# 64 elementwise products of a gated recurrence, on VectorE in place of GpSimd

## The chip, the core and the metric

The kernel runs on one NeuronCore of a Trainium2 chip. The core has a matrix engine (TensorE, PE in the profile; PEld is its weight load), a vector engine (VectorE, DVE), an activation engine (ScalarE, ACT), a general engine (GpSimd, POOL) and a queue engine (SyncE, SP) that here only issues DMA. Each engine works through its own list of instructions in a fixed order and waits on semaphores for the others. The metric is the device time of one execution, in microseconds (us), as the median of several runs.

## The reference

Two transformer blocks on 512 tokens of width 1024: the first with sparse attention, a gating unit and a mixture of experts, the second with stick-breaking attention, a gated linear recurrence and a second mixture of experts. The change lies in the recurrence of the second block. It has 4 heads of 128 and chunks of 128 tokens; cut to what matters:

```
def step(state, inp):
    qc, kc, vc, gc = inp
    bc = jnp.cumsum(gc, axis=2)
    diff = bc[:, :, :, None, :] - bc[:, :, None, :, :]
    decay = jnp.exp(jnp.where(causal, diff, -jnp.inf))
    scores = jnp.einsum('bhtd,bhsd,bhtsd->bhts', qc, kc, decay)
    o = einsum('bhts,bhsv->bhtv', scores, vc) + einsum('bhtd,bhdv->bhtv', qc * jnp.exp(bc), state)
    b_last = bc[:, :, -1, :]
    state = jnp.exp(b_last)[..., None] * state + einsum(
        'bhsd,bhsv->bhdv', kc * jnp.exp(b_last[:, :, None, :] - bc), vc)
    return state, o
```

The decay depends on the pair of positions and on the feature, so the scores are not one product of two matrices.

## The kernel before

The kernel is one program of five stages: first dense part, first experts, second dense part (`dense2`), second experts, final norm. A scheduler turns the Python code into the five lists of instructions; inside `dense2` the string `ORDER` only gives the order in which steps are handed to it, and it interleaves them by its own estimate. All weights come through SP's queue in a fixed order.

The step `L0` to `L3` of `dense2` is the function `levels(h)`, once for each head. It gets the scores of all four chunks (tile `sgf`) from seven products. For a level of half-length B, with `bc` the summed log decay, the tile `x` holds in every first half of 2B positions exp(ref - b) times the key and in every second half exp(b - ref) times the query, where ref is b at the end of the first half. Then x transposed times x holds the wanted scores for all pairs that are split by this level, and a mask picks them. A level is therefore a chain over engines: two subtractions on VectorE (lines 1916 and 1917), one exponential on ScalarE (through `act`, line 1755), two products (lines 1919 and 1920, with `kf` and `hq`), four products of 128x128x128 on TensorE into one PSUM bank (line 1924, tile `lv`; in fp32, so the trace has eight matmuls for four), and a masked copy from the bank into `sgf` on VectorE (line 1925). There is one such bank, so the next level's matmuls wait for this copy; three `x` buffers let the front of the chain run ahead.

After its levels each head makes the decayed queries `qe * q` (line 1930) and the decayed keys `kd * k` (line 1938), transposes the latter (`kt`, lines 1941 and 1942, copied to `kmt` by line 1944), and the step `A0` to `A3` (`across`) carries the state over the chunks. The steps beside it are the attention pairs `P0` to `P3` (`sb_pair`, where GpSimd also has masks, line 2014, and sums, line 2068), projections (`Q`, `G`, `I`; matmuls of lines 146 to 148 into `acc`), and the output product `W0` to `W3` (`back_first`). Each weight tile `wr` is split into a high half `wh` (ScalarE, line 135) and a low half `wl` (VectorE, line 138) before the matmuls may use it. `kmt` of head 1 ends the first half of the levels; levels 2 and 3 run after it without attention beside them.

Of the kernel before, what the change touches and what calls it, by code (L numbers as in the profile page):

```python
# [17 lines left out]
ALU = mybir.AluOpType  # L18
# [3 lines left out]
T = 512  # L22
# [1609 lines left out]
TM = T + NM  # L1632
# [93 lines left out]
def dense2(K, tc, A, router, dump=None):  # L1726

    nc = K.nc
# [8 lines left out]
    with st:  # L1737
# [15 lines left out]
        def act(out, in_, func, **kw):  # L1753

            i = nc.scalar.activation(out, in_, func, **kw)
            if table[0] is not None:
                after(K, i, table[0])
            acts.append(i)
# [7 lines left out]
        def bank(name, tag="ps"):  # L1766
            return (psz if tag == "z" else psp).tile([128, 512], F32, name=name, tag=tag, bufs=BANKS[tag])
# [18 lines left out]
        with tc.tile_pool(name="d2x0", bufs=1, side="right", reuse_waits="tile") as x0:  # L1786
# [18 lines left out]
            q = x0.tile([128, NT, D], F32, name="fq")  # L1805
# [85 lines left out]
        def chunks(ap):  # L1891
            return ap.rearrange("p (c s) -> p c s", s=128)

        def levels(h):

            lf = hp.tile([128, TM], F32, name=f"lf{h}", tag="lf", bufs=1)
            act(lf, sgf[:, h, :], AF.Ln, scale=lb1[:, h:h + 1], bias=lb[:, h:h + 1])
            bc = hp.tile([128, TM], F32, name=f"bc{h}", tag="bc", bufs=2)
            nc.vector.tensor_tensor_scan(bc[:, 0:T], first, lf[:, 0:T], 0.0, op0=ALU.mult, op1=ALU.add)
            nc.vector.tensor_tensor_scan(bc[:, T:TM], first[:, 1:1 + NM], lf[:, T:TM], 0.0, op0=ALU.mult, op1=ALU.add)  # L1900
            q, k = hq[:, h, :], kf[:, h, :]

            S = chunks(sgf[:, h, 0:T])
            ps = bank(f"dg{h}", "lv")
            for c in range(NT):
                s = slice(c * 128, (c + 1) * 128)
                nc.tensor.matmul(ps[:, s], k[:, s], q[:, s], start=True, stop=True)
            nc.vector.tensor_tensor(S, chunks(ps), K.ident[:, None, :].to_broadcast([128, NT, 128]), op=ALU.mult)
            for lg in range(7):
                B = 1 << lg  # L1910
                nb = T // (2 * B)
                v4 = lambda ap: ap.rearrange("p (n two b) -> p n two b", two=2, b=B)
                x = hp.tile([128, T], F32, name=f"x{h}{lg}", tag="X", bufs=3)
                b4, x4 = v4(bc[:, 0:T]), v4(x)
                ref = b4[:, :, 0, B - 1:B].to_broadcast([128, nb, B])
                nc.vector.tensor_tensor(x4[:, :, 0, :], ref, b4[:, :, 0, :], op=ALU.subtract)
                nc.vector.tensor_tensor(x4[:, :, 1, :], b4[:, :, 1, :], ref, op=ALU.subtract)
                act(x, x, AF.Exp)
                nc.gpsimd.tensor_tensor(x4[:, :, 0, :], x4[:, :, 0, :], v4(k[:, 0:T])[:, :, 0, :], op=ALU.mult)
                nc.gpsimd.tensor_tensor(x4[:, :, 1, :], x4[:, :, 1, :], v4(q)[:, :, 1, :], op=ALU.mult)  # L1920
                ps = bank(f"lv{h}{lg}", "lv")
                for c in range(NT):
                    s = slice(c * 128, (c + 1) * 128)
                    nc.tensor.matmul(ps[:, s], x[:, s], x[:, s], start=True, stop=True)
                nc.vector.copy_predicated(S, K.lev[lg][:, None, :].to_broadcast([128, NT, 128]), chunks(ps))

            qe = hp.tile([128, T], F32, name=f"qe{h}", tag="X", bufs=3)
            act(qe, bc[:, 0:T], AF.Exp)
            nc.vector.tensor_copy(ebs[:, h, :], chunks(qe)[:, :, 127])
            nc.gpsimd.tensor_tensor(q, qe, q, op=ALU.mult)  # L1930
            kd = hp.tile([128, T + 32], F32, name=f"kd{h}", tag="kd", bufs=1)
            nc.vector.memset(kd[:, TM:], 0.0)
            c3 = chunks(bc[:, 0:T])
            nc.vector.tensor_tensor(chunks(kd[:, 0:T]), c3[:, :, 127:128].to_broadcast([128, NT, 128]), c3,
                                    op=ALU.subtract)
            nc.vector.tensor_tensor(kd[:, T:TM], bc[:, TM - 1:TM].to_broadcast([128, NM]), bc[:, T:TM], op=ALU.subtract)
            act(kd[:, 0:TM], kd[:, 0:TM], AF.Exp)
            nc.gpsimd.tensor_tensor(kd[:, 0:TM], kd[:, 0:TM], k, op=ALU.mult)
            ps = bank(f"kt{h}", "lv")
            for c in range(NT - 1):  # L1940
                nc.tensor.transpose(ps[:, c * 128:(c + 1) * 128], kd[:, c * 128:(c + 1) * 128], K.ident)
            nc.tensor.transpose(ps[0:32, 384:512], kd[:, T:T + 32], K.ident)
            nc.scalar.activation(k[:, 0:384], ps[:, 0:384], AF.Copy)
            nc.vector.tensor_copy(kmt[:, h, :], ps[0:32, 384:512])
# [240 lines left out]
        for i in range(4):  # L2185
            steps[f"SK{i}"] = lambda i=i: col_meta(SK, lambda b: kT[b], i)
            steps[f"F{i}"] = lambda i=i: col_meta(HF, lambda b: kf[:, b, :], i)
            steps[f"P{i}"] = lambda i=i: sb_pair(i)
            steps[f"L{i}"] = lambda i=i: levels(i)
            steps[f"W{i}"] = lambda i=i: back_first(i)  # L2190
            steps[f"A{i}"] = lambda i=i: across(i)
# [151 lines left out]
```

## Time and profile before

| | us |
|---|---|
| median of 3 runs (1751.13 to 1752.42) | 1751.66 |
| the profiled execution | 1750.18 |
| its span from first to last instruction | 1748.4 |
| PE busy in the span | 1667.2 |
| DVE busy | 813.5 |
| ACT busy | 522.3 |
| POOL busy | 253.8 |

Busy times overlap: all engines run side by side. What lies outside the span (1.8 us) does not depend on the work. PE's busy time counts pipelined matmuls with modelled ends, so it is no measure of how well it is used.

### The profile page before, as it was taken

The numbers are of one execution on the slowest core, as the hardware profiler recorded it, in microseconds if no ns is written. First come the engines' busy times: TensorE is split into PE (matmuls) and PEld (weight loads), VectorE is DVE, ScalarE is ACT, GpSimd is POOL, SyncE is SP. The second block draws the span as 40 slices with busy tenths as digits, with TensorE's granted clock in tenths as the row PEclk, the third lists the DMA queues.
The fourth block names the chain that finished last, engine by engine and source line by source line (L and its number), as shares of the span: only waits on it lengthen the run. The fifth ranks groups of instructions, "written<-read, shape, count | busy, mean of one in ns | idle before, by whom it ended". The sixth has DMA issues, their size and how long they took to land. (4 is left out here: it accounts for less than half of the span.)

```text
span 1748.4 us, 22778 instructions
## 1 busy us (share of the span) xinstructions
PE 1667.2 (95%) x8932; PEld 1094.7 (63%) x8932; DVE 813.5 (47%) x1832; ACT 522.3 (30%) x896; POOL 253.8 (15%) x308
## 2 busy tenths in 40 slices
PE   8999999999999999999899999899999999999976
PEld 6877777787888745454487977688644344333423
DVE  6668865463346823322654378877611111211114
ACT  4333355662334210110425367634300000000012
POOL 0000111110211000000323257550000000000010
PEclk9999999999999999999999999999999999999998
DMA  4422222257334499999531220217499999999995
GB/s 139 134 73 73 73 73 61 60 175 241 95 100 144 184 420 407 420 420 407 218 109 49 73 72 1 73 37 297 187 419 420 419 420 420 418 420 420 419 419 225
DMA packets 112656, 403.72 MB, mean 231 GB/s; under 512 B 21950, under 2 KB 44478, under 8 KB 75936
## 3 DMA queue, kind: packets, MB, share of 16 engines
q1 hardware_dynamic: 101952, 376.60, 55.8%
q0 software_dynamic: 8880, 25.58, 3.8%
q8 instruction: 72, 1.18, 0.3%
q10 hardware_dynamic: 1712, 0.04, 0.1%
q14 instruction: 40, 0.33, 0.1%
HBM read 382.44 MB, written 27.26 MB: 234 GB/s over the span
## 5 line engine op out<-in xcount | busy, mean ns | idle before, releaser
L1533 PE MATMUL gg<-rg,xT 128*64 128x512 f32 x1536 | 372.7, 597 | 9.5 <-DMA rg<-in_w_expert_gate 5.0
L1533 PEld LDWEIGHTS gg<-rg,xT 128*64 128x64 f32 x1536 | 114.3, 136 | 210.6 <-issue 183.3
L1546 PE MATMUL py<-rg,aT 128*64 128x512 f32 x768 | 198.0, 604 | 20.9 <-DMA rg<-in_w_expert_down 20.9
L138 DVE TENSOR_TENSOR wl<-wr,wh 128x1024 fp32r<-128x1024 f32 (+2 forms) x114 | 141.0, 1238 | 136.8 <-ACT wh L135 135.3
L135 ACT ACTIVATE wh<-wr 128x1024 fp32r<-128x1024 f32 (+2 forms) x116 | 119.6, 1033 | 203.7 <-PE acc L148 113.1
L1546 PEld LDWEIGHTS py<-rg,aT 128*64 128x64 f32 x768 | 58.2, 138 | 141.5 <-issue 100.3
L1269 DVE SCALAR_TENSOR_TENSOR sg<-gg,gsl,sg 128x256 f32<-128x256 f32 (+1 forms) x32 | 19.7, 617 | 252.2 <-PE gg L1533 172.7
L146 PE MATMUL acc<-wh,xh 128*128 128x512 f32 (+3 forms) x312 | 121.3, 389 | 2.1 <-DVE xl L272 2.1
L1323 POOL DMA_INDIRECT yd<-ys,to x28 | 27.9, 998 | 655.4 <-DVE ys L1322 505.9
L148 PE MATMUL acc<-wl,xh 128*128 128x512 f32 (+3 forms) x312 | 119.9, 385 | 0.5 <-DVE wl L138 0.5
L147 PE MATMUL acc<-wh,xl 128*128 128x512 f32 (+3 forms) x312 | 118.8, 381 | 0.0
L1113 DVE TENSOR_TENSOR xT<-xp,gT 128x512 f32<-128x512 f32 x56 | 38.6, 690 | 152.7 <-PE xp L1110 150.3
L1280 ACT ACTIVATE aT<-ap 128x256 f32<-128x256 f32 (+1 forms) x32 | 15.7, 490 | 291.1 <-PE ap L1277 291.1
L1321 ACT ACTIVATE ys<-py,gsl 128x512 f32<-128x512 f32 x28 | 19.3, 688 | 257.1 <-PE py L1546 151.1
L1322 DVE TENSOR_SCALAR ys<-py,gsl 128x512 f32<-128x512 f32 x28 | 21.0, 751 | 135.9 <-PE py L1546 135.9
L146 PE MATMUL acc<-xh,wh 128*128 128x512 f32 x192 | 77.5, 404 | 0.0
L147 PE MATMUL acc<-xh,wl 128*128 128x512 f32 x192 | 76.7, 400 | 0.0
L148 PE MATMUL acc<-xl,wh 128*128 128x512 f32 x192 | 76.6, 399 | 0.0
L146 PEld LDWEIGHTS acc<-wh,xh 128*128 128x128 f32 x312 | 59.0, 189 | 17.7 <-issue 4.9
L148 PEld LDWEIGHTS acc<-wl,xh 128*128 128x128 f32 x312 | 59.0, 189 | 11.7 <-DVE wl L138 1.0
L146 PE MATMUL acc<-ah,wh 128*128 128x264 f32 (+1 forms) x192 | 63.6, 331 | 2.5 <-ACT wh L135 2.1
L147 PEld LDWEIGHTS acc<-wh,xl 128*128 128x128 f32 x312 | 59.2, 190 | 10.2
(752 smaller groups left out, 3476.3 us busy)
## 6 DMA issues: line engine op xcount, KB each, us to landing
rg<-in_w_expert_in SPq DMA_DIRECT2D x64, 1024.0 KB, 11.8
rg<-in_w_expert_gate SPq DMA_DIRECT2D x64, 1024.0 KB, 20.3
rg<-in_w_expert_up SPq DMA_DIRECT2D x64, 1024.0 KB, 20.2
rg<-in_w_expert_down SPq DMA_DIRECT2D x62, 1024.0 KB, 20.5
wr<-in_w_in SPq DMA_DIRECT2D x84, 512.0 KB, 3.6
rg<-in_w_expert_out SPq DMA_DIRECT2D x32, 1024.0 KB, 11.4
yd<-zeros POOLq DMA_DIRECT2D x2, 4096.0 KB, 24.9
yb<-yd POOLq DMA_DIRECT2D x14, 512.0 KB, 10.0
```

The source lines that it names most:

```text
L135: self.high = nc.scalar.activation(wh, raw, AF.Copy)
L138: self.low = low.tensor_tensor(wl, raw, f32(wh), op=ALU.subtract)
L146: nc.tensor.matmul(out, ah, bh, start=first, stop=False)
L147: nc.tensor.matmul(out, al, bh, start=False, stop=False)
L148: return nc.tensor.matmul(out, ah, bl, start=False, stop=last)
L1113: nc.vector.tensor_tensor(xT[:, k2 * 2:k2 * 2 + 2, :], ps, gT[:, kk:kk + 2, None].to_broadcast([128, 2, n]), op=ALU.mult)
L1269: K.gated = nc.vector.scalar_tensor_tensor(sg, ps_u, scale, sg, op0=ALU.mult, op1=ALU.mult)
L1321: nc.scalar.activation(y[:, 0:512], py[0], AF.Copy, scale=gate)
L1322: nc.vector.tensor_scalar(y[:, 512:D], py[1], gate, None, op0=ALU.mult)
L1323: nc.gpsimd.indirect_dma_start(yd, bass.IndirectOffsetOnAxis(ap=rows, axis=0), y, None, bounds_check=ROWS - 1, oob_is_err=False)
L1533: in_turn(nc.tensor.matmul(pss[i][64 * s:64 * s + 64, :], xT[kk // 4][:, kk % 4, c0 + 64 * s:c0 + 64 * s + 64], wt[2 * p + s, nm, kk // 4] ...
L1546: m = nc.tensor.matmul(py[q][64 * s:64 * s + 64, :], aT[:, f, 64 * s:64 * s + 64], wt[2 * p + s, second, f // 2][:, f % 2, q * 512:(q + 1) ...
```

## The change

Four lines name `nc.vector` where they named `nc.gpsimd`: 56 products of 128x256 (seven levels, two halves, four heads), four of 128x512 (line 1930) and four of 128x528 (line 1938). The computation is the same.

```diff
                 act(x, x, AF.Exp)
-                nc.gpsimd.tensor_tensor(x4[:, :, 0, :], x4[:, :, 0, :], v4(k[:, 0:T])[:, :, 0, :], op=ALU.mult)
-                nc.gpsimd.tensor_tensor(x4[:, :, 1, :], x4[:, :, 1, :], v4(q)[:, :, 1, :], op=ALU.mult)
+                nc.vector.tensor_tensor(x4[:, :, 0, :], x4[:, :, 0, :], v4(k[:, 0:T])[:, :, 0, :], op=ALU.mult)
+                nc.vector.tensor_tensor(x4[:, :, 1, :], x4[:, :, 1, :], v4(q)[:, :, 1, :], op=ALU.mult)
...
-            nc.gpsimd.tensor_tensor(q, qe, q, op=ALU.mult)
+            nc.vector.tensor_tensor(q, qe, q, op=ALU.mult)
...
-            nc.gpsimd.tensor_tensor(kd[:, 0:TM], kd[:, 0:TM], k, op=ALU.mult)
+            nc.vector.tensor_tensor(kd[:, 0:TM], kd[:, 0:TM], k, op=ALU.mult)
```

Every engine issues the same instructions as before, but for these 64. Their order differs on PE, DVE, ACT and POOL from the first head's levels to the end of the last head's, since the scheduler places the rest anew; SP's list is the same. Two places are shown. On DVE, in head 3, this is a stretch of the levels before the change (`x_10040` to `x_10076` are the tiles of levels 3 to 6, `lv_10034` to `lv_10058` the banks' contents of levels 2 to 4):

```order
L1925 COPY_PREDICATED sgf<-lv_4922,lv_10034 128x512
L1916 TENSOR_TENSOR x_10064<-bc_9995 128x8x32
L1917 TENSOR_TENSOR x_10064<-bc_9995 128x8x32
L138 TENSOR_TENSOR wl_10258<-wr_10255,wh_10257 128x1024
L1925 COPY_PREDICATED sgf<-lv_4923,lv_10046 128x512
L1916 TENSOR_TENSOR x_10076<-bc_9995 128x4x64
L1917 TENSOR_TENSOR x_10076<-bc_9995 128x4x64
L1952 COPY vmh_10313<-hvm 32x64
L1952 COPY vmh_10356<-hvm 32x64 x2
L1925 COPY_PREDICATED sgf<-lv_4924,lv_10058 128x512
```

And this is the same stretch of DVE after the change:

```order
L1925 COPY_PREDICATED sgf<-lv_4922,lv_10034 128x512
L1916 TENSOR_TENSOR x_10064<-bc_9995 128x8x32
L1919 TENSOR_TENSOR x_10052<-x_10052,kf 128x16x16
L1920 TENSOR_TENSOR x_10052<-x_10052,hq 128x16x16
L1917 TENSOR_TENSOR x_10064<-bc_9995 128x8x32
L1925 COPY_PREDICATED sgf<-lv_4923,lv_10046 128x512
L1916 TENSOR_TENSOR x_10076<-bc_9995 128x4x64
L1919 TENSOR_TENSOR x_10064<-x_10064,kf 128x8x32
L1920 TENSOR_TENSOR x_10064<-x_10064,hq 128x8x32
L1917 TENSOR_TENSOR x_10076<-bc_9995 128x4x64
L1925 COPY_PREDICATED sgf<-lv_4924,lv_10058 128x512
```

Between two masked copies DVE now has four instructions of a level, and the split of a weight (`wl_10258`) and the small copies that stood there have moved behind the last level. On PE, in the same head, the matmuls of levels 2 and 3 stood like this before (`acc` rows belong to the projection `I1`):

```order
L1924 MATMUL lv_10034<-x_10028 128x128 x4
L146 MATMUL acc_10106<-wh_10132,ah 128x256
L147 MATMUL acc_10106<-wh_10132,al 128x256
L148 MATMUL acc_10106<-wl_10133,ah 128x256
L146 MATMUL acc_10106<-wh_10132,ah 128x256
L147 MATMUL acc_10106<-wh_10132,al 128x256
L148 MATMUL acc_10106<-wl_10133,ah 128x256
L146 MATMUL acc_10106<-wh_10132,ah 128x256
L147 MATMUL acc_10106<-wh_10132,al 128x256
L1924 MATMUL lv_10046<-x_10040 128x128 x4
```

After the change all seven levels of this head stand together on PE, and the projection goes on behind them:

```order
L147 MATMUL acc_10107<-wh_10132,al 128x256
L1924 MATMUL lv_10010<-x_10004 128x128 x4
L1924 MATMUL lv_10022<-x_10016 128x128 x4
L1924 MATMUL lv_10034<-x_10028 128x128 x4
L1924 MATMUL lv_10046<-x_10040 128x128 x4
L1924 MATMUL lv_10058<-x_10052 128x128 x4
L1924 MATMUL lv_10070<-x_10064 128x128 x4
L1924 MATMUL lv_10082<-x_10076 128x128 x4
L148 MATMUL acc_10106<-wl_10133,ah 128x256
L146 MATMUL acc_10106<-wh_10132,ah 128x256
```

So PE has nothing to do between two levels of head 3, where it had seven to thirteen matmuls before; levels 2 to 5 of head 2 stand together in the same way. The half `wl_10133`, which the first row behind the levels needs, is made on DVE only just before the last masked copy.

## Rows read from the trace of the kernel before

**Rows 1.** Stretches: length; busy PE, PEld, DVE, ACT, POOL; PE clock, DMA share, GB/s.

```profile
1024.70:1124.70 100.00, 95.28 (x648) 69.89 (x646) 85.47 (x163) 71.53 (x144) 66.66 (x96) 1.00 0.12 38
1124.70:1173.50 48.80, 42.35 (x382) 39.92 (x383) 45.11 (x95) 18.22 (x32) 32.74 (x32) 0.97 0.14 44
1173.50:1252.00 78.50, 75.28 (x521) 68.87 (x520) 57.65 (x197) 30.89 (x59) 3.04 (x2) 1.00 0.58 228
1252.00:1748.00 496.00, 456.57 (x2125) 190.63 (x2123) 92.88 (x173) 45.82 (x85) 21.79 (x37) 0.99 0.96 396
1130.00:1140.00 10.00, 6.67 (x47) 6.32 (x47) 10.00 (x14) 4.16 (x6) 8.56 (x8) 0.89 0.18 52
1140.00:1150.00 10.00, 10.00 (x81) 9.64 (x81) 9.32 (x23) 3.00 (x7) 4.92 (x6) 0.94 0.01 2
```

**Rows 2.** A wait of SP's DMA queue, 1185 to 1270: us, times, longest.

```profile
SPq L974 <- PE acc L148: 27.2, 1, 27.2
```

**Rows 3.** Timelines of DVE and, in the last row, of POOL: start, us, engine, line.

```profile
1124.37 0.25 DVE L1944 COPY kmt<-kt 32x128 f32<-32x128 f32 x1
...
1125.64 0.41 DVE L1917 TENSOR_TENSOR x<-bc 128x256 f32<-128x256 f32 x1
1125.97 0.67 DVE L1908 TENSOR_TENSOR sgf<-dg,ident 128x512 f32<-128x512 f32 x1
...
1133.25 2.34 DVE L1899 TENSOR_TENSOR_SCAN bc<-first,lf 128x512 f32<-128x512 f32 x1
...
1137.43 1.20 DVE L138 TENSOR_TENSOR wl<-wr,wh 128x1024 fp32r<-128x1024 f32 x1
...
1171.51 0.75 DVE L1925 COPY_PREDICATED sgf<-lv,lv 128x512 f32<-128x512 uint8 x1 [1.11 <-PE lv L1924]
1173.57 0.74 DVE L1925 COPY_PREDICATED sgf<-lv,lv 128x512 f32<-128x512 uint8 x1 [1.31 <-PE lv L1924]
...
1133.01 1.50 POOL L1938 TENSOR_TENSOR kd<-kd,kf 128x528 f32<-128x528 f32 x1
```

**Rows 4.** Instructions by tile, all four heads: least, median and greatest ns.

```profile
L1916 DVE TENSOR_TENSOR x<-bc x28: 392/410/1119, 1025.1 to 1167.5; 128x256 f32<-128x256 f32 x28
L1917 DVE TENSOR_TENSOR x<-bc x28: 400/486/1221, 1025.4 to 1167.9; 128x256 f32<-128x256 f32 x28
L1919 POOL TENSOR_TENSOR x<-x,kf x28: 719/834/1799, 1027.5 to 1169.6; 128x256 f32<-128x256 f32 x28
...
L1899 DVE TENSOR_TENSOR_SCAN bc<-first,lf x4: 1217/1407/2342, 1023.8 to 1133.2; 128x512 f32<-128x512 f32 x4
...
L1934 DVE TENSOR_TENSOR kd<-bc x4: 659/1085/1333, 1035.7 to 1159.0; 128x512 f32<-128x512 f32 x4
L1936 DVE TENSOR_TENSOR kd<-bc x4: 152/480/824, 1038.3 to 1160.8; 128x16 f32<-128x16 f32 x4
```

**Rows 5.** Groups of DVE, 1124.7 to 1173.5: count, busy us, mean ns, idle before.

```profile
L1917 DVE TENSOR_TENSOR x<-bc 128x256 f32<-128x256 f32 x14 | 9.1, 647 | 0.0
L1916 DVE TENSOR_TENSOR x<-bc 128x256 f32<-128x256 f32 x14 | 6.7, 477 | 0.0
L138 DVE TENSOR_TENSOR wl<-wr,wh 128x1024 fp32r<-128x1024 f32 x4 | 6.0, 1491 | 0.0
L1934 DVE TENSOR_TENSOR kd<-bc 128x512 f32<-128x512 f32 x2 | 2.0, 996 | 0.0
L1936 DVE TENSOR_TENSOR kd<-bc 128x16 f32<-128x16 f32 x2 | 1.5, 766 | 0.0
```

**Rows 6.** The timeline of PE.

```profile
1133.38 0.28 PE L146 MATMUL acc<-wh,ah 128*128 128x256 f32 x1
...
1134.10 0.28 PE L146 MATMUL acc<-wh,ah 128*128 128x256 f32 x1
...
1136.36 1.13 PE L1924 MATMUL lv<-x 128*128 128x128 f32 x8 [1.98 <-DVE sgf L1925]
...
1173.29 0.49 PE L148 MATMUL acc<-wl,ah 128*128 128x256 f32 x2
```

## The prediction

> **What bounds the kernel now.** I read the stretches first. From 1252 us to the end the DMA engines are busy for 0.96 of the time at 396 GB/s and PE for 457 of 496 us [rows 1]: the last experts' weights stream at the rate that the queues give, so this stage ends a fixed time after its stream gets going. The stream can't get going on its own: in SP's queue the loads of the experts' weights stood 27.2 us behind matmuls of the dense stage [rows 2], whose weight buffers they take over. So what moves the end of PE's work in the dense stage moves the end of the kernel by as much, and nothing behind it takes a delay up; from 1173.5 to 1252 PE is busy for 75.3 of 78.5 us. The question is only when PE gets past the last level.
>
> Up to there the reader is to see two halves. In the first, 100 us with the attention pairs beside the levels, no engine is full: PE 95.3, DVE 85.5, ACT 71.5, POOL 66.7. In the second, 48.8 us with levels 2 and 3, DVE is busy for 45.1 and PE for 42.4 [rows 1], and PE's long waits are for the masked copy on DVE, as the 1.98 us ahead of 1136.36 [rows 6]. There DVE sets the time, and the change gives it more to do.
>
> **What DVE takes over.** A product of 128x256 is not on DVE before, but the subtraction is, with two inputs of the same size from SBUF: it takes 0.39 to 0.41 alone, and in a run of them the next begins 0.33 later [rows 3, 4]. The bounds are 0.33, and 0.65 if it were always blocked as the subtraction of line 1917 is on average [rows 5]; with nothing left on POOL in the second half I take 0.33. For 512 elements I take 0.6 (0.659 at least for line 1934 [rows 4], less the same overlap). Each half of the stage gets 28 products of levels and four large ones: 28 x 0.33 + 4 x 0.6 = 11.6 us.
>
> **What DVE gets back.** DVE and POOL hold each other up. The scan of line 1899 took 2.34 us at 1133.25, while POOL worked on decayed keys for 1.50 from 1133.01, where it takes 1.22 alone [rows 3, 4]. In the second half the mean over the least time of each group comes to: line 1917 14 x (0.647 - 0.400) = 3.5; line 1916 14 x (0.477 - 0.392) = 1.2; the four splits 4 x (1.491 - 1.20) = 1.2; the scan 1.1; line 1934 2 x (0.996 - 0.659) = 0.7; line 1936 2 x (0.766 - 0.152) = 1.2 [rows 3 to 5]. That is 8.9 us, and there all of POOL's work is what leaves it, so all of it comes back.
> The Trainium skill says of this ("SBUF — State Buffer", "Who interferes with whom") that a VectorE instruction with two SBUF inputs and a GpSimd instruction that reads SBUF block each other fully, whichever begins second. The trace agrees: 2.34 against 1.22, with 1.26 us of the 1.50 falling into it. By that rule the gain could be as large as all the time that the products were on POOL, and the sum below would come out faster; the rows give the 8.9.
>
> **The first half.** The same 11.6 us come onto DVE. I take the same 8.9 back as in the second half, so DVE has 2.7 us more in a half where it idles for 14.5 [rows 1]; POOL loses about 29 us of work (28 at a median of 0.83 [rows 4] and four of about 1.5 [rows 3]), so masks and sums of the attention pairs no longer queue behind products. PE's order there is nearly the old one. I count this half at nothing; if the idle time can't cover it, it costs 2.7, and more if the products, now in DVE's queue, wait for their exponential with attention work behind them (a rival). If POOL's shorter queue tells, it gains up to 4: of PE's 4.7 idle us little more than that can go.
>
> **The second half.** I sum DVE from the copy to `kmt` that ends at 1124.62 [rows 3] to the moment when PE goes on with `acc` behind the last level, 1173.29 before [rows 6], 48.7 us. In the new order that moment is the end of `wl_10133`, since the first row behind the levels needs it. DVE's work up to there: 45.1 as before, less 8.9, plus 11.6, plus the scan and one operation of 512 that now stand behind `kmt` instead of ahead of it (1.2 + 0.6), less one split that has moved behind the last level (1.2): 48.4. To this come DVE's own waits. A level in the new order is four instructions and the masked copy, 4 x 0.33 + 0.63 = 1.95; but the loop from one copy over PE's eight matmuls to the next copy takes 2.06 even where DVE idles for 1.31 of it (1171.51 to 1173.57 [rows 3]). With 11 such rounds in heads 2 and 3 that is 1.1; and I take 0.9 for the two `across` steps, whose square, root and norm go back and forth to ACT. DVE idles for 3.7 in this half before; 0 and 4 are the bounds of the 2.0. Sum 50.4, that is 1.7 us later than before (bounds -0.3 to +3.7).
>
> At that moment PE has done less than before. Counted in the two orders, the rows ahead of the last level hold 24 fewer matmuls of 128x256 (33 of the projection `I1` fall behind it, 9 come ahead). One is issued every 0.12 us (1133.38 to 1134.10, six steps [rows 6]): 24 x 0.12 = 2.9 us, which PE, full from here on, has to do later. That is the price of the bare block of seven levels: of 2.06 us a level PE works for eight matmuls, about 0.9.
>
> **The clock.** From 1130 to 1140 PE was busy for 6.67 us, and after those waits the granted clock was below full: 0.89 in these 10 us and 0.94 in the next 10 [rows 1], which is one spell at 1.2 in place of 2.4 GHz for (0.11 + 0.06) x 10 / 0.5 = 3.4 us; it costs half of that, 1.7. The new order has two sparse blocks, levels 2 to 5 of head 2 (some 8 us) and all of head 3 (some 14). I count one spell more, 1.7 us; bounds are one less and two more, -1.7 to +3.4.
>
> **Sum**: 0 + 1.7 + 2.9 + 1.7 = 6.3 us on the profiled execution's 1750.2: 1756.5. That execution is 1.5 below the median of the runs, so against the median 1751.7 + 6.3 = 1758.0.
>
> **The rivals.**
> *Nothing to measure.* The first half gains what POOL's queue held up (-4), or the 24 matmuls find their place in gaps behind the levels: 6.3 - 4 = 2.3, 1754. Against the second: PE is busy for 75.3 of 78.5 us there. For the first: POOL was busy for 67 us of 100 and 29 of them leave.
> *Faster.* The levels get shorter, as the change would have it: two products take 0.66 on DVE in a run against 1.44 on POOL at its best (0.719 each [rows 4]), and nothing blocks any more. PE's idle 6.4 us in the second half and the slow spell's 1.7 are what there is to win, 8.1; with half of it and a gain of 2 in the first half the time is 1746. It happens if DVE gets from `kmt` to `wl_10133` in less than 42.3 us (48.7 less the 2.9 of displaced work and the 3.5 of my bound). For it speaks that 14 levels took 48.7 us, 3.5 for each, where a round can take 2.06; against it that DVE's work of 48.4 us alone is more than 42.3.
> The Trainium skill's rule ("GPSIMD Engine Reference", "Performance versus the Vector engine") that VectorE is the engine for elementwise work is on this rival's side, with a factor of 1.96 at 2048 elements. The trace has 1.8 at 256 (0.719 to 0.392), and that this helps only an engine with time left is what the sum above weighs.
> *Slower still.* The products stand in DVE's queue and wait there for their exponential, and in the first half the attention's sums (lines 2006 to 2010 and 2025), on which ScalarE and PE wait, stand behind them. DVE's idle 14.5 us are the cover; with 8 of 28 products late by 0.7 (one exponential) it costs 5.6 more, 1763.6.
>
> **Chances.** Forecast (1755.5 to 1762) 0.42; slower still 0.13; nothing to measure 0.25; faster 0.20. A measurement of this kernel can tell 0.2%, 3.5 us, from no change: faster is below 1748.2, slower above 1755.2; so faster 0.20, same 0.25, slower 0.55. The range takes in the bounds of the first half (-4), the waits and the clock, and reaches into the rivals on both sides: 1747.5 to 1764.5; the forecast's own range is 1755.5 to 1762.
>
> **What would show it.** In the trace after: line 1919 on DVE at 0.39 to 0.41 in the second half, and lines 1916, 1917 and 1899 at their least there; masked copies of head 3 about 2.06 apart with PE idle for about 1 us between its groups; PE going on with `acc` 50 us after `kmt` of head 1, and the end of the `acc` rows 24 matmuls later than that; one or more further stretches with the clock below full. It is wrong if the first half, from the first scan to that `kmt` (100.8 us before), changes by more than 4 us, if the rounds are longer than 2.2 us, or if the experts' stream begins at another distance from the end of the dense stage's matmuls.

## The result, and the profile after

The changed kernel takes 1760.65 us (median of 5 runs, 1758.38 to 1760.71), the kernel before 1751.66 on the same chip: a ratio of 1.0053, with a 95% interval of 1.0042 to 1.0064. By the ratio that is 9.3 us slower, where 6.3 were forecast; the time lies in the forecast's own range, 1755.5 to 1762.

The two profiled spans differ by 10.5 us (1758.9 and 1748.4), but the first scan of the levels, before which nothing was moved, starts at 1025.07 after and at 1023.82 before. So 1.25 us belong to other stages and 9.2 to the change. These are the boundaries in the trace of after, first in the timeline of DVE, then in that of PE (start, us, engine, line).

```profile
1025.07 1.22 DVE L1899 TENSOR_TENSOR_SCAN bc<-first,lf 128x512 f32<-128x512 f32 x1
...
1124.68 0.27 DVE L1944 COPY kmt<-kt 32x128 f32<-32x128 f32 x1
```

```profile
1179.70 0.56 PE L148 MATMUL acc<-wl,ah 128*128 128x256 f32 x1
...
1247.24 0.39 PE L148 MATMUL acc<-wol,m2h 128*128 128x512 f32 x1
...
1263.08 0.65 PE L1533 MATMUL gg<-rg,xT 128*64 128x512 f32 x2
```

They are the first scan, `kmt` of head 1, PE going on behind the last level, the last `acc` matmul of the dense stage and the first matmul of the experts'. In the trace of before, the first scan and those two matmuls are these:

```profile
1023.82 1.22 DVE L1899 TENSOR_TENSOR_SCAN bc<-first,lf 128x512 f32<-128x512 f32 x1
...
1236.81 0.39 PE L148 MATMUL acc<-wol,m2h 128*128 128x512 f32 x1
...
1252.64 0.65 PE L1533 MATMUL gg<-rg,xT 128*64 128x512 f32 x2
```

The stretches of after between its boundaries, and two of 10 us in which the clock was low (the last runs 4.3 us beyond the second stretch), with the columns of [rows 1]:

```profile
1025.10:1124.95 99.85, 95.59 (x648) 69.51 (x647) 87.60 (x188) 69.21 (x142) 39.60 (x64) 1.00 0.10 33
1124.95:1179.70 54.75, 45.97 (x363) 42.12 (x361) 48.44 (x127) 21.05 (x36) 0.00 (x0) 0.86 0.09 30
1179.70:1263.10 83.40, 80.17 (x554) 73.52 (x553) 60.17 (x204) 32.04 (x62) 3.03 (x2) 0.99 0.59 227
1263.10:1758.90 495.80, 455.36 (x2117) 189.38 (x2116) 92.25 (x172) 45.22 (x84) 21.71 (x37) 0.99 0.96 396
1140.00:1150.00 10.00, 8.54 (x37) 7.86 (x38) 6.95 (x16) 2.09 (x4) 0.00 (x0) 0.55 0.08 21
1174.00:1184.00 10.00, 8.18 (x44) 7.54 (x43) 7.68 (x17) 2.10 (x4) 0.00 (x0) 0.66 0.25 68
```

The first half takes 99.9 us (100.8 before), the second 54.7 (48.7 before), the rest of the dense stage from 1179.70 to 1247.24 67.5 (63.5 before, 1173.29 to 1236.81): -0.9, +6.1 and +4.0. Behind that all is as it was: the experts' first matmul follows 15.84 us later (15.83 before, 1236.81 to 1252.64), and the rest takes 495.8 in both. SP's wait, which was 27.2 [rows 2], is nearly as long:

```profile
SPq L974 <- PE acc L148: 26.4, 1, 26.4
```

In the second half the mean granted clock is 0.86, that is (1 - 0.86) x 54.75 / 0.5 = 15.3 us at 1.2 GHz, in two spells: around 1140 to 1150, in head 2's block of levels and behind it (0.55), and from 1175 on, in head 3's and a little beyond (0.66). Before there was one of 3.4 us.

On DVE the products cost what the subtraction costs, and in the second half, where GpSimd has nothing left, nothing is blocked any more. In the first half GpSimd still has the attention's work, and there a product can take 1.40 us (at 1077.82, beside 1.37 of GpSimd from 1077.57). First instructions by tile over all heads (least, median, greatest ns, as in [rows 4]), then the groups of DVE in the second half (as in [rows 5], idle time and its releaser last):

```profile
L1919 DVE TENSOR_TENSOR x<-x,kf x28: 402/417/1403, 1031.0 to 1175.6; 128x256 f32<-128x256 f32 x28
...
L1899 DVE TENSOR_TENSOR_SCAN bc<-first,lf x4: 1214/1224/1225, 1025.1 to 1150.9; 128x512 f32<-128x512 f32 x4
...
L1936 DVE TENSOR_TENSOR kd<-bc x4: 158/166/168, 1040.9 to 1155.8; 128x16 f32<-128x16 f32 x4
```

```profile
L1925 DVE COPY_PREDICATED sgf<-lv,lv 128x512 f32<-128x512 uint8 x13 | 9.5, 730 | 4.9 <-PE lv L1924 4.9
L1917 DVE TENSOR_TENSOR x<-bc 128x256 f32<-128x256 f32 x14 | 5.9, 418 | 0.0
L1920 DVE TENSOR_TENSOR x<-x,hq 128x256 f32<-128x256 f32 x14 | 5.8, 418 | 0.0
L1919 DVE TENSOR_TENSOR x<-x,kf 128x256 f32<-128x256 f32 x14 | 5.8, 418 | 0.1
L1916 DVE TENSOR_TENSOR x<-bc 128x256 f32<-128x256 f32 x14 | 5.8, 413 | 0.0
L138 DVE TENSOR_TENSOR wl<-wr,wh 128x1024 fp32r<-128x1024 f32 x3 | 3.7, 1218 | 0.0
```

The block of head 3 on PE, where a row is now a whole level and nothing stands between two of them:

```profile
1170.98 1.13 PE L1924 MATMUL lv<-x 128*128 128x128 f32 x8 [0.92 <-ACT x L1755]
1173.02 1.13 PE L1924 MATMUL lv<-x 128*128 128x128 f32 x8 [0.92 <-ACT x L1755]
1175.07 2.02 PE L1924 MATMUL lv<-x 128*128 128x128 f32 x8 [0.91 <-DVE sgf L1925]
1178.00 2.05 PE L1924 MATMUL lv<-x 128*128 128x128 f32 x8 [0.91 <-DVE sgf L1925]
```

At full clock eight matmuls span 1.13 us and a round is 2.04; when the clock has fallen they span 2.02 and a round is 2.93. The idle 0.9 in each round stays, so a slow round is 0.89 longer, less than half of its length.

### The profile page after: what moved, and what is told of

The parts are those of the page before. It is cut to its first block, busy times and chain, and to the rows that moved or that the text cites. A ratio compares the mean times of both kernels' runs of the same rounds, so it can differ in the third digit from the quotient of the medians.

```text
span 1758.9 us, 22734 instructions
## 1 busy us (share of the span) xinstructions
PE 1675.9 (95%) x8930; PEld 1101.4 (63%) x8932; DVE 821.0 (47%) x1896; ACT 522.4 (30%) x896; POOL 192.6 (11%) x244
```

## The experiments

**Theory A (bare blocks).** DVE's list is full of products, so the splits of weights (line 138) that the projection needs move behind the levels. PE has nothing to issue between two levels of heads 2 and 3. Matmuls are displaced, and the clock falls. **Theory B (DVE's load).** DVE has more work in front of the last level, and the time follows it, whatever PE has between the levels. Every run is compared with the kernel before on the same chip, over all its runs; ratios carry 95% intervals.

In the first four runs the kernel before has a median of 1751.76 us, in the next four 1752.37, in the last four 1751.24.

**Level products alone.** Of the change, only these two lines:

```diff
-                nc.gpsimd.tensor_tensor(x4[:, :, 0, :], x4[:, :, 0, :], v4(k[:, 0:T])[:, :, 0, :], op=ALU.mult)
-                nc.gpsimd.tensor_tensor(x4[:, :, 1, :], x4[:, :, 1, :], v4(q)[:, :, 1, :], op=ALU.mult)
+                nc.vector.tensor_tensor(x4[:, :, 0, :], x4[:, :, 0, :], v4(k[:, 0:T])[:, :, 0, :], op=ALU.mult)
+                nc.vector.tensor_tensor(x4[:, :, 1, :], x4[:, :, 1, :], v4(q)[:, :, 1, :], op=ALU.mult)
```

> Only the 56 products of the levels (lines 1919 and 1920) go to VectorE; the eight large ones (lines 1930 and 1938) stay on GpSimd. Theory A (bare blocks: DVE's list, filled with products, puts the splits of the weights behind the levels, PE has nothing to issue between them, matmuls are displaced and the clock falls to 1.2 GHz): levels 2 to 5 of head 2 and six of the seven of head 3 still stand together on PE, so nearly all of the loss stays, 7 to 10 us over before, with some 14 us or more at half clock between 1130 and 1190. Theory B (DVE's added work sets the time, whatever stands on PE): 18.5 of the 23.2 us of products move, so 0.8 of the loss of 9, 7 us over before. The two differ in the clock, not in the time.

1763.17 us, ratio 1.0065 (1.0048 to 1.0082): all of the loss and, in the medians, more than that. In its second half the mean clock is 0.90:

```profile
1128.90:1182.40 53.50, 43.60 (x352) 39.70 (x351) 48.05 (x125) 19.76 (x36) 5.08 (x4) 0.90 0.10 30
```

This run shows which lines carry the loss; as expected, it doesn't separate the theories.

**Large products alone.** Of the change, only the other two:

```diff
-            nc.gpsimd.tensor_tensor(q, qe, q, op=ALU.mult)
+            nc.vector.tensor_tensor(q, qe, q, op=ALU.mult)
...
-            nc.gpsimd.tensor_tensor(kd[:, 0:TM], kd[:, 0:TM], k, op=ALU.mult)
+            nc.vector.tensor_tensor(kd[:, 0:TM], kd[:, 0:TM], k, op=ALU.mult)
```

> Only the eight large products (lines 1930 and 1938) go to VectorE. Theory A (bare blocks): PE has 5 to 14 matmuls between two levels of heads 2 and 3 as before, so no long spell at half clock (3.4 us or none) and a time within 2 us of before. Theory B (DVE's added work): 0.2 of the loss of 9, some 2 us over before.

1750.42 us, ratio 0.9992 (0.9983 to 1.0001), and the clock at 1.00 through both halves. As A has it; B's 2 us are outside the interval.

**I1's splits ahead.** The whole change, and in `proj_tok2`, which makes the projections of 256 columns (2816 is I1's first column):

```diff
-        ws.append(W.split(raw, 4, 256))
+        with K.tc.high_priority(offset=URGENT) if extra and c0 == 2816 else ExitStack(): ws.append(W.split(raw, 4, 256))
```

> The whole change, and the two splits of I1's weights (lines 135 and 138) are given to the scheduler with a higher priority, so DVE makes them ahead of head 3's levels; the work is the same. PE's order is that of the change up to head 3, whose levels now have 9 to 18 matmuls of the projection between them. Theory A (bare blocks): the 24 displaced matmuls (2.9 us) and the spell at half clock in head 3 (6.8 us, worth 2.9) come back, head 2's spell stays: some 3.3 us over before, about 1755. Theory B (DVE's added work): DVE has the same work in front of the last level, one split more, so the time stays 9 us over before, or above.

1751.85 us, ratio 1.0003 (0.9993 to 1.0012): nothing is left of the loss that can be measured. B falls, for DVE's work is the same. The stretches (columns as above) from the first scan to `kmt` of head 1, to PE going on, and to the last matmul of the dense stage, then head 2's block:

```profile
1026.20:1126.10 99.90, 95.60 (x648) 69.52 (x648) 87.64 (x188) 69.27 (x143) 39.66 (x65) 1.00 0.10 33
1126.10:1176.40 50.30, 46.76 (x428) 44.03 (x426) 47.98 (x128) 22.92 (x40) 0.00 (x0) 1.00 0.14 43
1176.40:1236.50 60.10, 58.72 (x391) 51.86 (x390) 46.20 (x141) 22.94 (x45) 0.00 (x0) 1.00 0.64 254
1140.00:1150.00 10.00, 7.97 (x63) 7.22 (x62) 9.92 (x22) 2.31 (x4) 0.00 (x0) 1.00 0.07 20
```

The second half is 4.4 us shorter than after the change with DVE as busy (47.98 to 48.44), and what follows is 7.4 shorter, mostly since PE got through 428 matmul records there in place of 363. More came back than expected (8.8 by the ratios for 5.7), because head 2's spell is gone too, in a block that is as bare as it was. That is one trace, and its execution is 2.4 us faster than the median: in the two traces the way from the first scan to the last `acc` matmul is 11.9 us shorter than after the change (210.3 for 222.2), by the ratios 8.8. The mean clock of the whole span is 0.986 to 0.991 in the twelve runs, so in some of them a spell may have come here too.

**The waits filled with idle work.** The whole change, and behind the matmuls of line 1924, for heads 2 and 3 (`dm` is one spare bank for each of these heads):

```diff
+                for c in range(3 if h > 1 else 0): nc.tensor.matmul(dm[:, c * 128:c * 128 + 128], x[:, c * 128:c * 128 + 128], x[:, 0:128], start=True, stop=True)
```

> The whole change, and in heads 2 and 3 each level is followed in the code by three products of 128x128x128 of its own x into a spare bank that nobody reads (42 products added, 84 matmuls, some 9.7 us of PE's time at full clock); DVE's list and the splits are not helped by it. Theory A (bare blocks, by the clock): PE is busy in its waits, the granted clock stays full between 1130 and 1190 (3.4 us or less at half), and 5 to 6 us come back although PE has 9.7 us more to do: some 3 to 4 us over before, 1755. If the loss is displaced work and DVE's alone, nothing comes back, and the time is 9 us over before or more, up to 18 if the added matmuls are on the path.

1755.50 us, ratio 1.0022 (1.0013 to 1.0031). This kernel does 84 matmuls more than the changed one and is 5.4 us faster (1.0053 - 1.0022 = 0.0031 of 1751.7). Its second half and head 2's block:

```profile
1124.80:1175.30 50.50, 49.33 (x458) 46.92 (x457) 48.85 (x129) 21.41 (x37) 0.00 (x0) 1.00 0.14 43
...
1140.00:1150.00 10.00, 10.00 (x85) 9.58 (x84) 9.55 (x23) 3.36 (x6) 0.00 (x0) 1.00 0.17 55
```

The clock stays at 1.00, and those 5.4 us are the nearest that a run comes to its price. This isn't peculiar to the profiled executions: the mean clock of the whole span is 0.985 to 0.987 in all five runs of the changed kernel and 0.989 to 0.992 in all eleven of this one. The other 3.3 that I1's splits gave back (1.0022 to 1.0003) are put down to real work in place of idle work.

**Heads 0 and 1 alone, heads 2 and 3 alone.** In `levels`, with `E` for `nc.gpsimd` in the four lines (and `h > 1` in the second run):

```diff
+            E = nc.vector if h < 2 else nc.gpsimd
```

> The products of heads 0 and 1 go to VectorE (lines 1919, 1920, 1930, 1938 for h < 2), those of heads 2 and 3 stay on GpSimd. Theory A (bare blocks): the second half has 5 to 14 matmuls between two levels as before, the first half has attention beside the levels, so the time is that of before or up to 1 us less: 1750 to 1752.5, and no spell of more than 3.4 us at half clock between 1120 and 1190. Theory B (DVE's added work sets the time wherever it comes): half of the products, half of the loss, some 4.5 us over before.

1755.11 us, ratio 1.0016 (1.0007 to 1.0025): 2.8 us slower, a miss for A as it was put and between the two theories. PE has matmuls between the levels and the clock is 1.00 in the second half, but that half takes 54.4 us:

```profile
1125.20:1179.60 54.40, 45.58 (x410) 42.06 (x408) 45.88 (x101) 21.97 (x39) 33.41 (x32) 1.00 0.16 49
```

The new order of the first half leaves head 2's scan behind `kmt`, as after the change, and here with slow products behind it. The timeline of DVE, and in that of PE the first level's matmuls with the wait ahead of them:

```profile
1124.90 0.27 DVE L1944 COPY kmt<-kt 32x128 f32<-32x128 f32 x1
...
1126.90 1.22 DVE L1899 TENSOR_TENSOR_SCAN bc<-first,lf 128x512 f32<-128x512 f32 x1
```

```profile
1134.07 0.60 PE L1924 MATMUL lv<-x 128*128 128x128 f32 x3 [1.89 <-POOL x L1920]
```

Before, that scan began ahead of `kmt`:

```profile
1123.23 1.22 DVE L1899 TENSOR_TENSOR_SCAN bc<-first,lf 128x512 f32<-128x512 f32 x1
```

So something that A lacked has a price here, and the order that the first half hands on may be it. That it is the late scan is not shown: with the large products alone the scan is behind `kmt` too (1126.87, `kmt` at 1126.38), with slow products behind it, and nothing is lost.

> The other half: the products of heads 2 and 3 go to VectorE, those of heads 0 and 1 stay on GpSimd. The six waits between the levels of head 3 are bare on PE, as in the whole change; between those of head 2 there are 0 to 17 matmuls. Theory A (bare blocks): nearly the whole loss less the spell in head 2, which is shorter or gone: 5 to 9 us over before, with at least one spell at half clock in head 3. Theory B (DVE's added work): half of the loss, some 4.5 us. If the loss arises in the first half, none.

1754.74 us, ratio 1.0020 (1.0011 to 1.0029): 3.5 us slower, less than the 5 to 9 that A expected, while B's 4.5 is inside the interval. The spell in head 3 is there, and longer than after the whole change: the mean clock from 1164 to 1180 is 0.57, which is 13.8 us at half clock. Here head 2's scan is ahead of `kmt` again (1124.67, `kmt` at 1125.81), and the second half takes only 49.3 us:

```profile
1126.10:1175.40 49.30, 42.41 (x357) 39.04 (x357) 45.64 (x121) 17.88 (x31) 0.00 (x0) 0.89 0.07 22
...
1164.00:1180.00 16.00, 12.42 (x57) 11.42 (x58) 11.55 (x26) 3.38 (x6) 0.00 (x0) 0.57 0.16 52
```

Head 3's last four levels run at half clock there. At 0.89 us for each, this half would take about 45.7 us at full clock, 3 less than before (an estimate): the products on VectorE do shorten the levels, and the bare block more than takes that back.

**The control.** The kernel before, with the one line of `proj_tok2` that puts I1's splits ahead.

> A control: the kernel before with nothing but the higher priority of the two splits of I1's weights. Its PE had matmuls between all levels already. Theory A (the splits matter to the change because its DVE list holds them back): no difference beyond 2 us. If the priority is worth something by itself, and what it gave back to the changed kernel was that and not the cure of the bare block, this kernel is 5 to 8 us faster than before.

1752.39 us, ratio 1.0005 (0.9996 to 1.0014). The priority is worth nothing measurable by itself; what it gave the changed kernel was the cure.

**More splits ahead.** The whole change, with the splits of I0 and I1 (in `proj_tok2`) and of W0 and W1 (in `back_first`) put ahead, at twice the priority of the run with I1's alone:

```diff
-        ws.append(W.split(raw, 4, 256))
+        with K.tc.high_priority(offset=1000) if extra and c0 in (2560, 2816) else ExitStack(): ws.append(W.split(raw, 4, 256))
...
-            wh, wl = W.split(W.load(A["w_out_2"][0], g * 256, 256, 0, 4), 4, 256)
+            raw = W.load(A["w_out_2"][0], g * 256, 256, 0, 4)
+            with tc.high_priority(offset=1000) if g in (0, 1) else ExitStack(): wh, wl = W.split(raw, 4, 256)
```

> The whole change with a higher priority (twice that of the run with I1's splits alone) for the splits of I0, I1, W0 and W1. PE has 7 to 30 matmuls between the first levels of head 2 and 9 to 15 between all of head 3; levels 3 to 6 of head 2 stay bare. Theory A (bare blocks): as with I1's splits alone or up to 2 us less: 1749.5 to 1752. Theory B (DVE's added work, or the order of the first half, which moves here too): 1755 or more.

1745.68 us, ratio 0.9968 (0.9958 to 0.9979): faster than both kernels, by more than A expected. Its control is the kernel before with this diff alone:

> A control to the fastest run so far: the kernel before, its products on GpSimd, with the same higher priority for the splits of I0, I1, W0 and W1. If the whole gain comes from the splits, this kernel is some 6 us faster than before too. If it takes both (DVE no longer blocked by GpSimd in levels whose waits are filled), it is within 2 us of before, as with I1's splits alone, since its PE had 4 to 19 matmuls between all levels already.

1752.92 us, ratio 1.0010 (1.0001 to 1.0019). So the gain takes both, the splits ahead and the products on VectorE. The second half with the products on VectorE, its stretch and the waits of PE in it (us, times, longest):

```profile
1126.70:1175.90 49.20, 45.89 (x426) 43.72 (x425) 47.99 (x128) 21.38 (x37) 0.00 (x0) 1.00 0.14 44
```

```profile
PE lv L1924 <- DVE sgf L1925: 1.8, 2, 0.9
PE lv L1924 <- ACT x L1755: 1.5, 2, 0.9
```

And with them on GpSimd:

```profile
1126.50:1177.70 51.20, 43.65 (x392) 40.02 (x392) 45.47 (x95) 19.17 (x33) 30.46 (x32) 1.00 0.14 42
```

```profile
PE lv L1924 <- DVE sgf L1925: 4.7, 4, 1.5
PE lv L1924 <- POOL x L1920: 2.8, 5, 1.2
```

PE waits 3.3 us for levels with the products on VectorE and 7.5 with them on GpSimd, where the subtraction of line 1917 takes 701 ns on average against 418.

Three mixtures were run with the same splits ahead, to see which products make the gain: with `E = nc.vector if h < 2 else nc.gpsimd` as above, with lines 1930 and 1938 alone on VectorE, and with line 1919 alone.

> Products of heads 0 and 1 on VectorE, of heads 2 and 3 on GpSimd, with the higher priority for the splits of I0, I1, W0 and W1. The first half's order is that of the fastest run, the second half has 6 to 26 matmuls in all waits, the four of head 2 that are bare there among them. If bare waits are what is left to win, 2 to 4 us below that run, 1742 to 1744; if DVE is better off without products on GpSimd beside it in the second half, above it, 1747 to 1750.

1750.20 us, ratio 0.9991 (0.9982 to 1.0000).

> Only the eight large products on VectorE, with the higher priority for the splits of I0, I1, W0 and W1. All waits of heads 2 and 3 have 6 to 18 matmuls. If the gain of the fastest run is that of filled waits, it comes here too: 1745 to 1748. If it takes the level products on VectorE, this stays near the run with the large products alone, 1750.

1751.00 us, ratio 0.9992 (0.9983 to 1.0001).

> Of the two products of a level the first (line 1919) on VectorE, the second (line 1920) and the large ones on GpSimd, with the higher priority for the splits of I0, I1, W0 and W1. PE has 3 to 25 matmuls in all waits of heads 2 and 3. If filled waits alone decide, 1744 to 1747. If GpSimd beside DVE costs what the rows of before show (blocking of some 9 us in the second half with two products a level there, half of it with one), 1749 to 1752.

1747.30 us, ratio 0.9978 (0.9969 to 0.9987). In all three every wait of heads 2 and 3 has matmuls in it and the clock is full there. So filled waits are not enough: with the second half's products on GpSimd, or only the large ones on VectorE, nothing measurable is won. With one of two on VectorE the gain is two thirds in the medians, but that interval overlaps the one with all products on VectorE (0.9958 to 0.9979), so these two aren't told apart.

## Why the prediction was right, and where a size was off

**Passing on one to one**: right. 15.84 to 15.83 us and 495.8 to 495.8 behind the dense stage; SP's wait 26.4 to 27.2.

**What DVE takes over and gets back**: right. Line 1919 is at 418 ns in the second half, the next begins 0.33 later; lines 1916 and 1917 are at 413 and 418 against 477 and 647 [rows 5], the scan at 1.22 against 2.34, line 1936 at 0.17. DVE's work up to PE's going on was put at 48.4 us and is 48.44. By the rule of the Trainium skill ("SBUF — State Buffer", "Who interferes with whom") as I read it, up to all of GpSimd's product time could have come back; the measured work bears out the 8.9 of the rows in the second half. In the first, where GpSimd keeps the attention's work, DVE is busy for 2.1 us more than before (87.6 to 85.5), where 2.7 were put.

**The first half**: 0 forecast, -0.9 measured. GpSimd's shorter queue (39.6 us busy for 66.7 [rows 1]) bought little: PE's idle time there went from 4.7 us [rows 1] to 4.3.

**The second half**: +1.7 forecast, as 50.4 us from `kmt` to PE's going on. With the clock full it is 50.3 (I1's splits ahead) and 50.5 (waits filled), so DVE's and the rounds' part was right, and the rounds are 2.04. After the change it is 54.7. DVE's waits, put at 2.0, are 6.3, 4.9 of them for PE's matmuls of a level, the longest 2.17 at half clock. The scan behind `kmt`, which the sum counted, is there (1126.68, `kmt` at 1124.68).

**The displaced matmuls**: 2.9 forecast. The end of the dense stage is 4.0 us further from PE's going on, of which about 1 is the half clock that lasts beyond 1179.70, so some 3 are this term. The filled waits against I1's splits give 3.3.

**The clock**: this is the term that was mis-sized. "I count one spell more, 1.7 us", with 3.4 as the upper bound; the two sparse blocks were named, but each was given the length that the one spell of before had. In fact each lasted longer, and beyond its block: some 10 us from about 1141 and some 7 from 1175, that is 15.3 us in the second half and about 2.2 beyond it (0.79 from 1179.7 to 1185), against 3.4 before. Half of the difference of 14.1 would be 7.0; in a bare round it costs less than half (0.89 of 2.93 us), and the run with filled waits measures 5.4. The rounds and the clock were kept as separate terms, but a slow round is 2.57 to 2.93 us, over the 2.2 that the prediction had named as a sign of being wrong. With the 5.4 the sum is -0.9 + 1.7 + 2.9 + 5.4 = 9.1, where 9.0 to 9.3 are measured; so close an agreement is luck, since the 5.4 is uncertain by 2.5.

**The rivals.** *Nothing to measure* needed some 4 us from the first half, which gave 0.9, or gaps for the displaced matmuls behind the levels, where the rest of the stage took 4.0 us longer. *Slower still* came close in size (1763.6) but not by its mechanism: the first half, where attention's sums were to wait, is shorter than before. *Faster* had a true core: without GpSimd beside it a level does get shorter, as the two kernels with the splits ahead show. What it lacked is that the scheduler has to find PE something to issue meanwhile. So the change has either sign: slower by 0.53% in the order that the scheduler gave it, and, with four steps' splits ahead, 1745.7 us with the products on VectorE where it is 1752.9 with them on GpSimd (each against its own runs of before: 0.9968 and 1.0010).
The Trainium skill ("Perfetto Trace Analysis", "Optimizing Scalar/DVE Operations") says that with a full VectorE offloading work to GpSimd may make sense, and that it might not help since the two share a port. That pair of runs agrees with the second half of that: with the products on VectorE, DVE is busy for 48.0 of 49.2 us, and taking work back from GpSimd is what helped.

**What stays open.** The filled waits' 5.4 us are uncertain by some 2.5 us either way (half widths of 0.0011 and 0.0009 in the two ratios), and that kernel's order differs from the changed one's in more than the added matmuls; in the two traces the dense stage from the first scan on is 6.9 us shorter. What costs the 2.8 us of heads 0 and 1 alone was not found. How the splits of I0, W0 and W1 share in the last gain wasn't separated either.

## What to carry to other kernels

When work moves to another engine, look at what it pushes back in that engine's list and at who was fed by that: here the split of one weight, 1.2 us, for which 33 matmuls of a projection had to wait. A chain that leaves PE idle can cost twice, once for the work that could have stood there (here some 3 us) and once for the clock (here some 5). Before a change of engine is given up, fill the waits by the order and time it again: here the pair with the splits ahead gave the opposite sign of the first run.

## What was not expected of the hardware

The same bare block of head 2 has the clock at 0.55 from 1140 to 1150 after the change and at 1.00 with I1's splits ahead, although its levels start 2.04 to 2.07 us apart in both up to there (1136.43, 1138.50, 1140.55 and 1137.59, 1139.66, 1141.70). With more splits ahead, four rounds of head 2 are as bare, and the clock is at 1.00 from 1140 to 1150 too. So the order alone doesn't say whether a block of some 8 us, with PE idle for 0.9 of every 2 us, loses the clock; the spell in head 3, a block of 15 us, came in all three profiled kernels that had it bare. Matmuls whose results nobody reads made a kernel 5.4 us faster (2.5 either way).
